# A decoder trunk on one core: the second mixer's background steps of both queues on every second tick

## The chip, the cores and the metric

The kernel runs on one core of one Trainium2 chip. The metric is the device time of one execution in microseconds (us), and lower is better. The time before is the median of three runs.

## The reference, cut to what matters

The reference is one inference step of a two-layer decoder trunk: a Mamba-2 mixer, an MLP with squared ReLU, an HGRN2 mixer, a second MLP. 512 new prompt tokens and 8 sequences of 4 sampled tokens pass through together (544 token columns), width 1024, all in fp32 precision. The change is in the HGRN2 mixer, whose core is this:

```python
proj = u @ w_in                                  # (L, 4 * 1024): q, f, v, g
q = silu(q); k = (1 - lb) * sigmoid(-f)          # 8 heads of 128 x 128
# per token t and head: S_t = diag(f_t) S_{t-1} + k_t v_t^T,  o_t = S_t^T q_t   (in chunks)
o = group_rmsnorm(o) * silu(g)
x = x + o @ w_out
```

The sampled tokens start from a given state for each sequence and return the new one.

## The kernel before

All activations lie transposed: 8 tiles of 128 rows by 544 columns. A weight product is done in three passes (high part by high, high by low, low by high) in fp32r, each in two halves of 272 columns. So one unit of 128 outputs over a depth of 1024 takes 8 x 3 x 2 = 48 matmuls of 272 columns. Weights come by DMA on SyncE's queue into three `raw` buffers; ScalarE (L199) and VectorE (L200) split them into `whi` and `wlo`.

**Foreground and background.** The weight products are the foreground. Whatever else needs TensorE is written as Python generators, and each `yield` in one names how many ticks pass until its next step. `products` calls `tick()` after each 12 matmuls of 272 columns, that is 4 ticks for a unit. A tick takes one off the count of the first generator in each of two queues, and runs a step of it where the count has come to zero or below. `drain(name)` runs what is left of a generator at once, with no foreground between. The first mixer and the first MLP use the same queues before.

**The second mixer** (`hgrn`, L1179). For each of 8 heads `head` makes four units (q, f, v, g). After f it puts `levels(h)` into queue 0. That has eight steps: seven levels with block lengths s = 1, 2, 4, 8, 16, 32, 64 (tile `pa`, matmuls on column strips of 32 or 64 of the array, L1249 and L1268; the first two have an extra pair for the sampled tokens, L1256) and one step `values` (transposes into `pv` and `pvs`). When it ends it puts `states(h)` into queue 1, again eight steps: `pk` (transposes of K), `pS` (chunk states; half a pace until the next step), `pz` (the sampled tokens' old states, column strips of 32, L1362; half a pace until the next), `po` (the outputs, with `pzs`, then squares, mean, Newton steps for the root, scaling), `pn` twice (new states, L1396, added on VectorE in L1399), the store of the new states, and `pt` (transposes of the output, then the gate and the split into the operands `oh`, `ol`). One pace is 1.8 ticks for levels and 1.6 for states.

After the eight heads (128 ticks) comes the output product `pho`: half 0 uses heads 0 to 3 (8 products of 24 matmuls, 16 ticks); then `drain("hs7")` and half 1 with heads 4 to 7 (head 7 is the last operand in each product). Two accumulators (`acc`) take turns in all of these, and four one-bank PSUM tiles (`mx`) serve the background.

A planner turns the program into one order for each engine when the kernel is built: it takes instructions by priority in the order written, except that one whose inputs it does not expect in time is put behind later ones that are ready. `add_to_x` and some others have a higher priority. On the chip each engine then keeps its order.

Of the kernel before, what the change touches and what calls it, by code (L numbers as in the profile page):

```python
# [41 lines left out]


PACE = (1.1, 0.9, 1.4, 0.8)
PACE_LEVELS, PACE_STATES = 1.8, 1.6

U_SSD_IN = 0
U_SSD_OUT = U_SSD_IN + 40
# [53 lines left out]
def trunk(ctx: ExitStack, tc: tile.TileContext, io):  # L102
# [37 lines left out]

    ready = {}
    loaded = {("u", i): t for i, t in enumerate(first)}
    state = {"load": 2, "conv": 0}
    loads = [("u", u) for u in range(U_MLP)]
    jobs = [(("u", u), u) for u in range(U_MLP)]

# [141 lines left out]
    def unit(u):  # L288
        return take(("u", u))
# [3 lines left out]
    queues = [[], []]  # L293

    def tick():
        for q in queues:
            if q:
                q[0][1] -= 1
                while q and q[0][1] <= 0:
                    step(q)  # L300

    def step(q):
        try:
            q[0][1] += next(q[0][0])
        except StopIteration:
            left = q.pop(0)[1]
            if q:
                q[0][1] += left
# [7 lines left out]
    def drain(name):  # L316
        for q in queues:
            while any(e[2] == name for e in q):
                step(q)
# [5 lines left out]
    def products(ps, w, ops, first, last, c0=0, step=P, run=0):  # L325

        n = len(ops)
        order = [(k, j) for k in range(n) for j in range(3)]
        run = run or (4 if "w" in sp else 0)
        if run:  # L330

            order = [(k, j) for k0 in range(0, n, run) for js in ((0, 1), (2,)) for k in range(k0, min(k0 + run, n)) for j in js]
        for i, (k, j) in enumerate(order):
            oh, ol = ops[k]
            a, o = ((w[0], oh), (w[0], ol), (w[1], oh))[j]
            for h in range(2):
                nc.tensor.matmul(  # L337
                    ps[:, h, :HF], block(a, c0 + k * step), o[:, h * HF : (h + 1) * HF],
                    start=(first and i == 0), stop=(last and i == len(order) - 1),
                )  # L340
            if i % 6 == 5:
                tick()

    def acc_tile(name):
        return psb.tile([P, 2, 512], F32, tag="acc", name=name)
# [4 lines left out]
    def v3(t):  # L350
        return t.rearrange("p (a b) -> p a b", a=2)
# [73 lines left out]
    def add_to_x(m, ps, then):  # L425
        with tc.high_priority():
            nc.vector.tensor_tensor(v3(x[m]), ps[:, :, :HF], v3(x[m]), ADD)
        if then is not None:
            then(m)


    def ssd(then):
# [393 lines left out]
        def dt_product():  # L826

            wd = pool.tile([P, KT, NS], F32, tag="E", bufs=2, name="wd")
            nc.vector.tensor_tensor(
                wd, wdt, vec[:, V_NMIX0 : V_NMIX0 + KT].unsqueeze(2).to_broadcast([P, KT, NS]), MUL  # L830
            )
            pd = acc_tile("pd")
            for i in range(2):
                for h in range(2):
                    for c in range(4):
                        k = 4 * i + c
                        nc.tensor.matmul(
                            pd[c * NS : (c + 1) * NS, h, :HF], wd[:, k, :], x[k][:, h * HF : (h + 1) * HF],
                            start=(i == 0), stop=(i == 1), tile_position=(0, c * NS),
                        )  # L840
                tick()
            pdx = pool.tile([P, 640], F32, tag="xs", bufs=5, name="pdx")
            nc.vector.tensor_tensor(v3(pdx[:, :T]), pd[:, :, :HF], v3(rb), MUL)
            nc.gpsimd.tensor_copy(
                pdx[:, T:640].rearrange("p (a b) -> p a b", b=NS), pdx[:, NP_:T].unsqueeze(1).to_broadcast([P, 3, NS])
            )
            return pdx
# [122 lines left out]
    def mlp(name, plan, v0, then, last=False):  # L970
# [105 lines left out]
        def seventh(name_, u):  # L1076
# [11 lines left out]
            for k in range(4):  # L1088
                oh, ol = ops_[name_, k]
                for j, (w, o) in enumerate(((hi, oh), (hi, ol), (lo, oh))):  # L1090
                    nc.tensor.matmul(  # L1091
                        ps, block(w, k * P), o, start=(name_ in ("p1", "p2", "q7") and k == 0 and j == 0),
                        stop=(k == 3 and j == 2), skip_group_check=name_ in ("n6", "n5", "p3", "q4"),
                    )
            tick()
            release(1)
            keep = {"p1": "s1", "n6": "sv", "n5": "sw"}.get(name_)
# [81 lines left out]
    def hgrn(then):  # L1179
# [263 lines left out]

        sc = slice(NP_, T)
        u = U_HGRN_IN
        ops = [[pool.tile([P, T], F32R, tag=f"o{c}{h}", bufs=1, name=f"o{c}{h}") for c in "hl"] for h in range(8)]
        for h in range(8):
            head(u, h)
            u += 4
        for half in range(2):  # L1450
            if half:
                drain("hs7")
            for mp in range(4):
                w = unit(u)
                u += 1
                for i in range(2):
                    ps = acc_tile(f"pho{half}_{mp}_{i}")
                    products(ps, w, ops[4 * half : 4 * half + 4], True, True, i * P, 2 * P)
                    add_to_x(2 * mp + i, ps, then if half == 1 else None)
        es.close()  # L1460

    CH = (0, 91, HF - 91)
# [47 lines left out]
    ssd(pre_norm(V_NMLP0))  # L1510
    mlp("m0", plans[0], V_NMLP0, pre_norm(V_NMIX1))
    hgrn(pre_norm(V_NMLP1))
    mlp("m1", plans[1], V_NMLP1, last_norm, True)

# [111 lines left out]
def _build(arrays):  # L1626
    import concourse.bacc as bacc

    nc = bacc.Bacc("TRN2", target_bir_lowering=False, num_devices=1)
    io = {n: nc.dram_tensor(f"in_{n}", v.shape, mybir.dt.from_np(v.dtype), kind="ExternalInput").ap() for n, v in arrays.items()}  # L1630
    for n, s in _OUT.items():
        io[n] = nc.dram_tensor(f"out_{n}", s, F32, kind="ExternalOutput").ap()
    with tile.TileContext(nc) as tc:
        trunk(tc, io)
    return nc
# [22 lines left out]
```

## Time and profile before

| | |
|---|---|
| median of 3 runs | 1518.04 us (1516.65 to 1519.53) |
| the profiled execution's own time | 1517.97 us |
| its span | 1516.2 us |
| busy share of the span | PE 99%, PEld 95%, DVE 83%, ACT 58%, POOL 12% |
| granted TensorE clock, mean | 0.994 of 2.4 GHz |
| the second mixer (first product to last) | 816.05 to 1147.80 us |

PE is TensorE's matmul side and PEld its weight loads, DVE is VectorE, ACT ScalarE, POOL GpSimd, SP SyncE. L337 is a line of the kernel. Matmuls are pipelined and their records overlap, so the time that TensorE spends on something is read from the distances between starts. In the rows `ps<-uh,whi x2` is one pair of foreground matmuls; pairs that follow each other start 0.25 us apart.

### The profile page before, as it was taken

The page shows a single profiled execution, that of the slowest core. Times are in us where ns is not written, and L with a number is a line of the kernel's source. Part 1 is how long each engine was busy: PE and PEld are TensorE (multiplying, and loading weights), DVE is VectorE, ACT ScalarE, POOL GpSimd, SP SyncE. Part 2 cuts the span into 40 slices and gives each one's busy share as a digit, 9 for nine tenths or more (in the row PEclk, how much of TensorE's full clock was granted, in tenths as well). Part 3 has the DMA queues.
Part 4 walks back from the last instruction along what each step waited for, and adds up shares of the span by engine and source line. Part 5 has one row for each costly group of instructions (what it writes and reads, how often), then busy time and mean ns, then how long its engine had stood idle before and what let it go on. Part 6 is the DMA issues. An engine that isn't in the chain of part 4 may idle for free. (4 is left out here: it accounts for less than half of the span.)

```text
span 1516.2 us, 33224 instructions
## 1 busy us (share of the span) xinstructions
PE 1495.4 (99%) x13144; PEld 1440.3 (95%) x13144; DVE 1261.5 (83%) x2532; ACT 882.3 (58%) x1740; POOL 188.0 (12%) x273
## 2 busy tenths in 40 slices
PE   9999999999999999999999999999999999999997
PEld 7998989898999999999999999999999999999996
DVE  7879798978777989888898788888877989888895
ACT  5685766757346658575676333333336758576673
POOL 3211011110012111111110000000002111111101
PEclk9999999999999999999999999999999999999998
DMA  6366557574466667564754232233228666575741
GB/s 199 106 192 169 148 140 203 130 223 115 114 178 135 141 161 183 145 183 131 191 131 130 74 99 87 87 98 105 86 86 202 133 168 180 140 181 140 184 123 66
DMA packets 105789, 215.46 MB, mean 142 GB/s; under 512 B 16481, under 2 KB 36865, under 8 KB 105633
## 3 DMA queue, kind: packets, MB, share of 16 engines
q1 hardware_dynamic: 81328, 170.24, 34.7%
q0 software_dynamic: 23040, 41.95, 17.3%
q8 instruction: 103, 1.69, 0.5%
q10 hardware_dynamic: 1264, 1.14, 0.2%
q14 instruction: 54, 0.43, 0.1%
HBM read 196.12 MB, written 17.18 MB: 141 GB/s over the span
## 5 line engine op out<-in xcount | busy, mean ns | idle before, releaser
L199 ACT CAST whi<-raw 128x512 fp32r<-128x512 f32 x194 | 119.4, 617 | 212.0 <-PE ps L337 154.6
L200 DVE TENSOR_TENSOR wlo<-raw,whi 128x512 fp32r<-128x512 f32 x194 | 133.8, 691 | 30.8 <-ACT whi L199 28.0
L188 POOL DMA_DIRECT2D v<-in_W x94 | 83.0, 1038 | 463.6 <-DVE fl_p L200 134.0
L337 PE MATMUL ps<-uh_s,whi 128*128 128x272 f32 x576 | 124.3, 297 | 2.5 <-DVE BC L518 2.4
L337 PE MATMUL ps<-ul_s,whi 128*128 128x272 f32 x576 | 120.2, 290 | 0.0
L337 PE MATMUL ps<-uh,whi 128*128 128x272 f32 x512 | 112.6, 300 | 0.0
L337 PE MATMUL ps<-ul,whi 128*128 128x272 f32 x512 | 106.5, 289 | 0.0
L337 PE MATMUL ps<-uh,wlo 128*128 128x272 f32 x512 | 106.3, 289 | 0.0
L337 PEld LDWEIGHTS ps<-uh_s,whi 128*128 128x128 f32 x576 | 90.5, 189 | 8.5 <-issue 6.9
L337 PEld LDWEIGHTS ps<-ul_s,whi 128*128 128x128 f32 x576 | 90.9, 189 | 0.2
L200 DVE TENSOR_TENSOR fl_p<-raw,fh_p 128x512 fp32r<-128x512 f32 x94 | 64.1, 689 | 28.9 <-ACT fh_p L199 25.3
L337 PE MATMUL ps<-uh_s,wlo 128*128 128x272 f32 x576 | 86.4, 290 | 0.0
L337 PEld LDWEIGHTS ps<-uh,whi 128*128 128x128 f32 x512 | 80.8, 189 | 3.7 <-issue 1.4
L337 PEld LDWEIGHTS ps<-ul,whi 128*128 128x128 f32 x512 | 80.4, 189 | 0.0
L337 PEld LDWEIGHTS ps<-uh,wlo 128*128 128x128 f32 x512 | 80.0, 188 | 0.0
L199 ACT CAST fh_p<-raw 128x512 fp32r<-128x512 f32 x94 | 57.6, 620 | 37.9 <-PE pp L1091 19.9
L337 PEld LDWEIGHTS ps<-uh_s,wlo 128*128 128x128 f32 x576 | 78.1, 190 | 1.1 <-issue 0.8
L223 ACT CAST whi<-raw 128x512 fp32r<-128x512 f32 x66 | 40.6, 618 | 49.4 <-PE ps L337 19.6
L511 DVE SCALAR_TENSOR_TENSOR cacc<-pre,vh,cacc 128x568 f32<-128x568 f32 x72 | 57.8, 803 | 7.6 <-ACT cacc L509 7.1
L337 PE MATMUL po<-yh,whi 128*128 128x272 f32 x256 | 55.5, 297 | 1.2 <-ACT yh L199 1.2
L1091 PE MATMUL pp<-m_tl,fh_n 128*128 128x272 f32 x192 | 55.3, 288 | 0.0
L1091 PE MATMUL pc_q<-m_th,fh_q 128*128 128x272 f32 x192 | 55.3, 288 | 0.0
(480 smaller groups left out, 5156.0 us busy)
## 6 DMA issues: line engine op xcount, KB each, us to landing
raw<-in_W SPq DMA_DIRECT2D x175, 512.0 KB, 4.0
v<-in_W SPq DMA_DIRECT2D x94, 256.0 KB, 4.1
v<-in_W POOLq DMA_DIRECT2D x94, 256.0 KB, 5.6
wlo<-in_W POOLq DMA_DIRECT2D x66, 256.0 KB, 6.2
a<-in_W SPq DMA_DIRECT2D x47, 256.0 KB, 4.3
w<-cum_d SPq DMA_DIRECT2D x16, 512.0 KB, 6.9
st<-in_ssm_in SPq DMA_DIRECT2D x16, 512.0 KB, 4.6
out_ssm_s<-st SPq DMA_DIRECT2D x16, 512.0 KB, 6.6
```

Source lines behind the costliest of these rows:

```text
L188: nc.gpsimd.dma_start(raw[:, c : c + 512], io["W"][u + 1][:, :512], accum_op=ADD)
L199: nc.scalar.copy(hi, raw)
L200: (eng or nc.vector).tensor_tensor(lo, raw, hi.bitcast(F32), SUB)
L223: nc.scalar.copy(hi[a], c)
L337: nc.tensor.matmul(ps[:, h, :HF], block(a, c0 + k * step), o[:, h * HF : (h + 1) * HF], start=(first and i == 0), stop=(last and i == len( ...
L511: nc.vector.scalar_tensor_tensor(acc, pre[:, i : i + 568], vh[:, wc + 24 * i : wc + 24 * i + 1], acc, MUL, ADD)
L1091: nc.tensor.matmul(ps, block(w, k * P), o, start=(name_ in ("p1", "p2", "q7") and k == 0 and j == 0), stop=(k == 3 and j == 2), skip_group ...
```

## The change

The two paces become 2 ticks. `state` gets a count of ticks, and a beat: `tick()` still counts down each queue at every tick, but runs steps only when the count of ticks, which goes on from the kernel's start, is a multiple of the beat. The beat is 1 outside, and 2 from the first head to the end of the output product. `drain` is as before.

```diff
-PACE_LEVELS, PACE_STATES = 1.8, 1.6
+PACE_LEVELS, PACE_STATES = 2, 2
...
-    state = {"load": 2, "conv": 0}
+    state = {"load": 2, "conv": 0, "ticks": 0, "beat": 1}
...
     def tick():
+
+        state["ticks"] += 1
         for q in queues:
             if q:
                 q[0][1] -= 1
-                while q and q[0][1] <= 0:
+                while q and q[0][1] <= 0 and state["ticks"] % state["beat"] == 0:
                     step(q)
...
         u = U_HGRN_IN
+        state["beat"] = 2
...
                     add_to_x(2 * mp + i, ps, then if half == 1 else None)
+        state["beat"] = 1
         es.close()
```

## Rows read from the trace of the kernel before

**Rows 1.** Who TensorE waited for in the whole execution (us in total, times, longest).

```profile
PE po L337 <- ACT yh L199: 1.2, 2, 0.6
PE po L337 <- DVE yl L200: 0.6, 1, 0.6
PE pp L1091 <- ACT sw L1101: 0.3, 1, 0.3
```

**Rows 2.** Busy time of each engine in the second mixer; the last three numbers are granted clock, DMA share and GB/s.

```profile
816.05:1147.80 331.75, 331.66 (x3925) 311.55 (x3924) 268.93 (x734) 120.85 (x249) 9.19 (x23) 1.00 0.30 96
```

**Rows 3.** The chain of work around head 1's first level: start, us, what.

```profile
859.79 3.71 PE ps L337 x28
863.51 0.58 PE pa L1249 x32
```

**Rows 4.** TensorE in order of time around one level step (s = 16) that stands alone: start, us, line, tile.

```profile
882.88 0.41 PE L337 MATMUL ps<-uh,wlo 128*128 128x272 f32 x2
883.22 0.46 PE L1249 MATMUL pa<-q,K 128*32 128x32 f32 x32
883.61 0.52 PE L337 MATMUL ps<-uh,whi 128*128 128x272 f32 x2
883.96 0.41 PE L337 MATMUL ps<-ul,whi 128*128 128x272 f32 x2
```

**Rows 5.** The same around the first level (s = 1) of head 0, which stands alone: last pair ahead, first matmuls, second pair behind.

```profile
834.81 0.41 PE L337 MATMUL ps<-uh,wlo 128*128 128x272 f32 x2
835.16 0.65 PE L1249 MATMUL pa<-q,K 128*32 128x64 f32 x32
...
836.19 0.41 PE L337 MATMUL ps<-ul,whi 128*128 128x272 f32 x2
```

**Rows 6.** The same around `pz` of head 0, which stands alone.

```profile
868.39 0.41 PE L337 MATMUL ps<-uh,wlo 128*128 128x272 f32 x2
868.73 0.65 PE L1362 MATMUL pz<-hst,qm 128*32 128x128 f32 x16
...
869.39 0.50 PE L337 MATMUL ps<-uh,whi 128*128 128x272 f32 x2
869.73 0.41 PE L337 MATMUL ps<-ul,whi 128*128 128x272 f32 x2
```

**Rows 7.** The same around a first level and a `pz` that stand together.

```profile
900.55 0.41 PE L337 MATMUL ps<-uh,wlo 128*128 128x272 f32 x2
...
901.47 0.60 PE L1362 MATMUL pz<-hst,qm 128*32 128x128 f32 x13
...
902.42 0.41 PE L337 MATMUL ps<-ul,whi 128*128 128x272 f32 x2
```

**Rows 8.** The last pair ahead and the second pair behind, first of a level (s = 4) with `po` right behind it, then of a `po` that stands alone.

```profile
870.73 0.41 PE L337 MATMUL ps<-uh,wlo 128*128 128x272 f32 x2
...
874.24 0.41 PE L337 MATMUL ps<-ul,whi 128*128 128x272 f32 x2
...
903.43 0.41 PE L337 MATMUL ps<-uh,wlo 128*128 128x272 f32 x2
...
906.36 0.42 PE L337 MATMUL ps<-ul,whi 128*128 128x272 f32 x2
```

**Rows 9.** The start of the mixer, TensorE and VectorE: the norm's second step, the first evacuation that needs it, and the first pair of the third unit.

```profile
826.42 1.20 PE L382 MATMUL hn_pr<-ident,nwr 128*128 128x128 f32 x10
...
828.21 0.72 DVE L1228 TENSOR_TENSOR qz<-ps,hn_rb 128x544 f32<-128x544 f32 x1 [0.46 <-ACT hn_rb L385]
...
830.54 0.42 PE L337 MATMUL ps<-uh,whi 128*128 128x272 f32 x2
```

**Rows 10.** The last head's output around the border of the two halves: TensorE, then VectorE, then ScalarE, each in order of time.

```profile
1115.44 0.52 PE L337 MATMUL pho<-oh,whi 128*128 128x272 f32 x2
...
1117.06 0.39 PE L1396 MATMUL pn<-vm,kq 128*128 128x512 f32 x1
1117.29 0.41 PE L337 MATMUL pho<-oh,whi 128*128 128x272 f32 x2
...
1122.04 0.60 PE L1406 MATMUL pt<-ident,o 128*128 128x128 f32 x4
...
1122.74 0.52 PE L337 MATMUL pho<-oh,whi 128*128 128x272 f32 x2
...
1115.91 0.82 DVE L1386 TENSOR_REDUCE oms<-o 128x5 f32<-128x640 f32 x1 [1.26 <-ACT o L1384]
...
1120.23 0.69 DVE L1389 TENSOR_TENSOR o<-po,nwr 128x512 f32<-128x512 f32 x1
...
1121.51 0.33 DVE L1392 TENSOR_SCALAR o<-pzs,nwr 32x128 f32<-32x128 f32 x1
...
1124.04 0.73 DVE L1410 SCALAR_TENSOR_TENSOR g<-pt,vec,g 128x512 f32<-128x512 f32 x1
...
1124.96 0.65 ACT L199 CAST oh<-g 128x544 fp32r<-128x544 f32 x1 [2.36 <-DVE g L1411]
```

**Rows 11.** SyncE's queue at the same place: the last store of new states and the next weight load.

```profile
1124.13 1.42 SPq L1401 DMA_DIRECT2D out_hgrn_s<-hst  x1
1131.11 0.33 SPq L178 DMA_DIRECT2D raw<-in_W  x1
```

**Rows 12.** Busy time of each engine and the granted clock around the end of the first mixer (columns as in rows 2).

```profile
435.00:445.00 10.00, 8.69 (x48) 7.82 (x49) 5.94 (x10) 4.39 (x7) 4.22 (x5) 0.83 0.91 243
```

## The prediction

> **What bounds the kernel.** I read the page first, then who TensorE waited for, then the stage that the change touches, and there TensorE in order of time. No line in the list of TensorE's waits belongs to the second mixer; some of the list that lie nearest before it are in [rows 1]. In the mixer TensorE is busy for 331.66 of 331.75 us at a clock of 1.00, VectorE for 268.93 and ScalarE for 120.85 [rows 2]. So the mixer's time is the sum of what stands in TensorE's order. Of that the foreground is 40 units of 48 matmuls (8 heads of 4, and the output product as 8) = 1920 matmuls, or 960 pairs of 0.25 us: 240 us. The other 90 us or so are background steps. The change deletes no instruction. It can move the time in three ways only: what TensorE loses where it changes between foreground and background, a new wait of TensorE, or a weight that comes late.
>
> The planner already keeps TensorE from waiting: head 1's first level is due 12 matmuls after the level before it, and stands behind 28 [rows 3], since its inputs are not there sooner.
>
> **Which steps meet, before and after.** This is counted from the code. Before the mixer 449 ticks have passed: 217 in the first mixer (two units of 4; one in the product for dt; 36 units of 4; 32 output products of 2) and 232 in the MLP (8 up and 8 down units of 4, and 24 pairs with 7 products of one each). 449 is odd, so the beat falls on the mixer's odd ticks. Before the change, two heads take 32 ticks and interrupt the foreground 23 times, because paces of 1.8 and 1.6 drift against each other: `pk`, `pS`, `po` or `pn` meet a level at times, and `pz` stands alone in one head and with the first level in the next. After it each head is the same, eight visits in 16 ticks: (s1, pk), (s2, pS), (s4, pz, po), (s8, pn), (values, pn), (s16, store), (s32, pt), (s64). `pz` and `po` fall together because half a pace is now one tick, and steps run at every second. So 16 visits for two heads instead of 23.
>
> **What a visit costs.** From the last pair ahead to the second pair behind, less two pairs (0.50):
> - A level alone: 883.96 - 882.88 - 0.50 = 0.58, of which 0.09 is ahead of its first matmul (883.22 - 882.88 - 0.25) and 0.10 behind the first pair after it [rows 4].
> - A level with `po` behind it: 874.24 - 870.73 - 0.50 = 3.01; `po` alone 906.36 - 903.43 - 0.50 = 2.43 [rows 8]. 0.58 + 2.43 = 3.01: meeting saves nothing. The change from column strips to the whole array is paid at `po` instead of at the foreground.
> - First level alone 0.88 [rows 5], `pz` alone 0.84 [rows 6], the two together 902.42 - 900.55 - 0.50 = 1.37 [rows 7]: meeting saves 0.35. Both work on column strips.
> - Behind `pz` the foreground's first pair takes 869.73 - 869.39 - 0.25 = 0.09 too long [rows 6]. With `po` behind it that is saved.
>
> The Trainium skill (TensorEngine Tiling, Key Properties) states that a change of tiling mode drains TensorE, while another tile of the same mode does not. The rows agree: 0.09 and 0.10 around a level, nothing saved with an untiled neighbour, something with a tiled one. By that rule alone the gain would be one pair of changes in every second head, 0.19 x 3.5 = 0.7 us.
>
> **Gain.** After the change `pz` meets s4 in every head, before it met a level in every second. The meeting saves between 0.19 (0.09 + 0.10) and 0.35, and the border to `po` another 0.09: 0.28 to 0.44 per head, against 0.35 / 2 = 0.17 before. Over 7 heads that is (0.11 to 0.27) x 7 = 0.8 to 1.9 us. I take **-1.3 us**. The other meetings count as nothing, by rows 8.
>
> **The start.** The norm's second step `hn_pr` was due at tick 6 and is now run at tick 7, 12 matmuls or 1.5 us later. The third unit needs the first unit's accumulator, which `qz` frees. It ended at 828.21 + 0.72 = 828.93 and the third unit began at 830.54 [rows 9]. 1.5 us later it ends at 830.43: the slack falls from 1.6 us to 0.1. I take **+0.1**, from 0 to 0.7 (one ScalarE cast of 0.65, as in rows 10, ahead of the copies).
>
> **The border of the halves.** Here is the cost. Head 7's states start at tick 139 instead of 136, and go at 2 ticks a step. Before, `po` ran at tick 140, both `pn` in ticks 141 and 143, and only the store and `pt` were left for `drain`. Now `pz` and `po` run at tick 143, one tick ahead of the border, and `drain` has `pn`, `pn`, the store and `pt` with no foreground between them. The operand of head 7 was ready at 1124.96 + 0.65 = 1125.61, which is 10.2 us after the foreground came back behind `po` at 1115.44 [rows 10]. In this stretch VectorE also did its other work. Without it the chain is: 0.47 until the reduction, 0.85 for it, 2.4 for the scalar and 11 Newton steps, 1.0 for the two scalings, 0.9 for the transposes, 0.9 for the gate, 0.9 for the cast, about 7.4 us (estimated from the same stretch). What TensorE can do meanwhile: 12 foreground matmuls (1.5), two `pn` (1117.29 - 1117.06 = 0.23 each), the first 18 matmuls of both open accumulators, which need heads 4 to 6 only (36 x 0.125 = 4.5), and `pt` (0.8): 7.3 us. So TensorE waits between 0.1 (bare chain) and 2.9 us (VectorE as loaded as before). VectorE is 81% busy in the mixer [rows 2] and the eight adds of `pn` fall into the same stretch, but their order is the planner's. I take **+1.5**. Late next is the split of x behind the first products of half 1, which has its own accumulators' time as cover.
>
> **What else moves.** On SyncE's queue the store of new states and the state loads move by a few ticks, with weight loads behind them. The last store waits for the last `pn` add; the next weight load came 5.6 us after that store was through (1124.13 + 1.42 to 1131.11) [rows 11], so a store 2 to 3 us later is covered. Without cover it would cost its delay once. GpSimd is busy for 9.19 us of 331.75 [rows 2] and its copies keep their distance to their readers. Four `mx` tiles are enough for (s4, pz, po with pzs); where one is not free, the planner puts foreground there, as in rows 3. `po` behind `pz` needs ScalarE's copy for `pzs` only, 1.6 us later. Each of these: 0.
>
> **Sum.** -1.3 + 0.1 + 1.5 = +0.3 us. The profiled execution's 1517.97 becomes 1518.3; its median is 1518.04, which makes 1518.3 as well.
>
> **Rivals.**
> - *Slower: the border is not covered.* If the planner leaves `pn`, `pn`, `pt` in the order written, TensorE waits for the scaled output: 1121.84 - 1115.44 = 6.4 us after `po`, less 1.5 and 0.5, is 4.4, and behind it only one accumulator's 2.3 us covers a chain of some 3. That is about 4.5 to 5 us. Such a pause can also cost clock: around 435 to 445 us, where TensorE waited 1.2 + 0.6 us [rows 1], the granted clock was 0.83 in the mean [rows 12], which is part of it at the lower level of 1.2 GHz, and 10 x 0.17 = 1.7 us of work lost. The Trainium skill (TensorE: Matmul & The Clock Gate, HAM oscillation) names this as the mechanism: idle gaps bring the gate back to half rate; rows 12 agree. -1.3 + 4.8 + 1.7 = +5.2: 1523 us. It decides from a wait of 4.4 us. Against it: in rows 3 the planner did fill.
> - *Faster: each visit saved is worth a whole pair of changes.* 7 visits fewer for two heads, 24.5 in all, at 0.19 is 4.7 us: 1513.4 us. Against it speak rows 8. Half of it would do to be faster, with the border covered.
> - *It does nothing that can be seen*: both terms under 0.5 us, 1517.5 to 1518.5. That lies within the forecast.
>
> **Numbers.** Forecast (small gain, small wait) 0.75; the slower rival 0.15; the faster one 0.10. The bound of what can be told is 0.2%, 3.0 us. Slower by more needs a wait above 4.3 us, or one of 2.6 with lost clock; faster by more needs three times my gain and no wait. So faster 0.09, same 0.75, slower 0.16. Range: from 1518.04 - 1.9 less 1.0 for the runs' own scatter (1516.65 to 1519.53), 1515.2, to 1518.04 - 0.8 + 0.7 + 2.9 + 1.0 = 1521.8; I stop at 1522.2, which takes in the start of the slower rival.
>
> **What would show it.** In the changed profile: 8 visits in each head; (s4, pz, po) at 3.4 to 3.6 us where the three alone make 0.58 + 0.84 + 2.43 = 3.85; a first pause of TensorE between 828 and 832 of at most 0.7; a pause of 0 to 3 us at the border behind a run of first products of both accumulators; the mixer's stretch at 332 us. The prediction is wrong if TensorE waits inside the heads (for `zi` or a PSUM tile), if the clock falls at the border, or if other stages change by more than 1 us.

## The result: slower by 0.3%, and the profile after

The changed kernel takes 1522.55 us (median of 7 runs, 1521.54 to 1526.24) against 1518.04 us before (the median of seven runs too, and the same as of the three ahead of the prediction). The ratio is 1.0032, with a 95% interval of 1.0022 to 1.0042. That lies just above the range (1522.2), between the forecast and the slower rival, "the border is not covered" (1523): the rival's lost clock came, its long wait did not. The profiled execution took 1522.55 us with a span of 1520.8 us and a mean granted clock of 0.993.

Line numbers of the changed kernel are two higher than before: the products are L339, the levels L1251, `pz` L1364, `po` L1377 and L1379, the adds of `pn` L1401, the scaling L1391, `pt` L1408, the gate L1412.

Where TensorE waited in the whole execution: of the lines that name steps of the second mixer there were none before [rows 1], and now there are three (engine, line, who was waited for: us in total, times, longest).

```profile
PE pho L339 <- ACT oh L199: 1.5, 1, 1.5
PE pt L1408 <- DVE o L1391: 1.3, 1, 1.3
PE pn L1398 <- ACT vt L1315: 0.4, 1, 0.4
```

The first two stand at the border of the halves. This is TensorE there in order of time, after the change (start, us, line, tile; in brackets how long it was idle before, and for whom):

```profile
1118.51 0.65 PE L1364 MATMUL pz<-hst,qm 128*32 128x128 f32 x16
...
1121.24 0.40 PE L1382 MATMUL pzs<-vs,sats 32*32 32x128 f32 x2
1121.58 0.73 PE L1398 MATMUL pn<-vm,kq 128*128 128x512 f32 x2
1122.14 0.41 PE L339 MATMUL pho<-oh,whi 128*128 128x272 f32 x2
...
1126.41 0.41 PE L339 MATMUL pho<-oh,wlo 128*128 128x272 f32 x2
1128.15 0.63 PE L1408 MATMUL pt<-ident,o 128*128 128x128 f32 x4 [1.33 <-DVE o L1391]
1128.71 0.24 PE L1409 MATMUL pts<-ident,o 32*128 32x32 f32 x1
1130.46 1.27 PE L339 MATMUL pho<-oh,whi 128*128 128x272 f32 x4 [1.51 <-ACT oh L199]
1131.53 0.66 PE L339 MATMUL pho<-ol,whi 128*128 128x272 f32 x2
```

Three things are to be seen. Both `pn` follow `pzs` at once: no foreground stands between `po` and the drain. The 36 first products of both open accumulators (18 pairs, the first at 1122.14, the last at 1126.41) do fill a part, as the prediction had it. Then TensorE waits for the scaled output and for the operand `oh`, and behind the second wait a pair takes 0.45 us and more (1131.53 to 1131.98, where the next one starts) instead of 0.25. The windows show why (busy time of PE, PEld, DVE, ACT, POOL; then clock, DMA share, GB/s):

```profile
1118.00:1130.00 12.00, 9.62 (x83) 8.20 (x81) 8.45 (x30) 2.78 (x7) 0.00 (x0) 1.00 0.26 92
1130.00:1134.00 4.00, 3.54 (x15) 3.31 (x16) 1.87 (x3) 1.22 (x3) 0.00 (x0) 0.57 0.00 0
1134.00:1152.50 18.50, 18.50 (x150) 18.50 (x149) 15.21 (x24) 11.90 (x21) 0.00 (x0) 1.00 0.39 125
```

For 4 us after the waits the clock granted was 0.57 in the mean, most of it at the lower level of 1.2 GHz: 4 x 0.43 = 1.7 us of work lost. Before, the whole mixer had 1.00 [rows 2]. So the border costs 1.33 + 1.51 + 1.7 = 4.5 us.

From the first product to the start of the last `pho` matmul the mixer takes 334.02 us, before 330.74: +3.28. (The end at 1147.80 in the table of before lies behind that, in the first products of the next stage.) The stretch can be cut in two where the heads end and the border begins, at the last pair ahead of head 7's `pS`: up to there both kernels have run the same background steps. These are the first product and that pair, first before, with what follows the pair, then after:

```profile
816.08 0.41 PE L337 MATMUL ps<-uh,whi 128*128 128x272 f32 x2
...
1108.13 0.42 PE L337 MATMUL pho<-oh,wlo 128*128 128x272 f32 x2
1108.38 1.05 PE L1352 MATMUL pS<-vt,kt 128*128 128x128 f32 x8
1109.19 0.50 PE L337 MATMUL pho<-oh,whi 128*128 128x272 f32 x2
1109.53 0.41 PE L337 MATMUL pho<-ol,whi 128*128 128x272 f32 x2
```
```profile
817.58 0.41 PE L339 MATMUL ps<-uh,whi 128*128 128x272 f32 x2
...
1114.27 0.41 PE L339 MATMUL pho<-oh,wlo 128*128 128x272 f32 x2
```

After the change 24 more pairs of foreground, 6.0 us, stand ahead of it, since `pS` comes four ticks later. So the heads have changed by (1114.27 - 817.58) - 6.0 - (1108.13 - 816.08) = -1.36 us, which is what the visits saved, and the rest, with the border in it, by 3.28 + 1.36 = +4.64, near the 4.5 above.

The other 1.3 us of the difference between the two profiled executions (4.58 in all) stand elsewhere. In the first mixer a step that began at 160.42 us before begins at 161.88, although TensorE's order up to there is the same in both. The windows there, before and then after (columns as above):

```profile
145.00:170.00 25.00, 21.58 (x163) 20.92 (x164) 18.10 (x40) 9.65 (x18) 2.01 (x4) 0.93 0.79 243
```
```profile
145.00:170.00 25.00, 21.57 (x151) 20.92 (x151) 16.69 (x38) 8.55 (x16) 2.01 (x4) 0.86 0.79 243
```

TensorE is busy for the same time and gets less done in it, by a clock of 0.86 against 0.93: 25 x 0.07 = 1.75 us. In eight other kernels, none of which changes that part, the same step began between 159.85 and 164.51 us. Up to that step the order of all 1180 of TensorE's matmuls is the same in the ten traces. That is scatter between executions and no effect of the change. How much of the loss in the other runs stands outside the mixer, no run shows. So kernels are compared below by the ratio of their times and by the stretch of the second mixer alone.

### The profile page after: what moved, and what is told of

Read it like the earlier page. It is cut to its first block, busy times and chain, and to the rows that moved or that the text cites. A ratio compares the mean times of both kernels' runs of the same rounds, so it can differ in the third digit from the quotient of the medians.

```text
span 1520.8 us, 33217 instructions
## 1 busy us (share of the span) xinstructions
PE 1496.7 (98%) x13144; PEld 1441.0 (95%) x13144; DVE 1267.8 (83%) x2532; ACT 883.0 (58%) x1740; POOL 191.0 (13%) x273
## 5 line engine op out<-in xcount | busy, mean ns | idle before, releaser
L339 PE MATMUL ps<-uh_s,whi 128*128 128x272 f32 x576 | 124.6, 298 | 2.5 <-DVE BC L520 2.4
L339 PE MATMUL ps<-ul_s,whi 128*128 128x272 f32 x576 | 120.7, 291 | 0.0
L339 PE MATMUL ps<-uh,whi 128*128 128x272 f32 x512 | 110.7, 297 | 0.0
L339 PE MATMUL ps<-ul,whi 128*128 128x272 f32 x512 | 106.0, 288 | 0.0
L339 PE MATMUL ps<-uh,wlo 128*128 128x272 f32 x512 | 105.8, 288 | 0.0
L339 PEld LDWEIGHTS ps<-uh_s,whi 128*128 128x128 f32 x576 | 90.7, 190 | 8.5 <-issue 6.9
L339 PEld LDWEIGHTS ps<-ul_s,whi 128*128 128x128 f32 x576 | 91.3, 190 | 0.3
L339 PE MATMUL ps<-uh_s,wlo 128*128 128x272 f32 x576 | 87.3, 292 | 0.0
L339 PEld LDWEIGHTS ps<-uh,whi 128*128 128x128 f32 x512 | 80.3, 188 | 3.0 <-issue 1.2
L339 PEld LDWEIGHTS ps<-ul,whi 128*128 128x128 f32 x512 | 80.2, 188 | 0.0
L339 PEld LDWEIGHTS ps<-uh,wlo 128*128 128x128 f32 x512 | 80.1, 188 | 0.0
L339 PEld LDWEIGHTS ps<-uh_s,wlo 128*128 128x128 f32 x576 | 79.0, 192 | 1.1 <-issue 0.8
L339 PE MATMUL po<-yh,whi 128*128 128x272 f32 x256 | 55.4, 297 | 1.2 <-ACT yh L199 1.2
```

Of the source, the lines that this page charges most:

```text
L339: nc.tensor.matmul(ps[:, h, :HF], block(a, c0 + k * step), o[:, h * HF : (h + 1) * HF], start=(first and i == 0), stop=(last and i == len( ...
```

## The experiments

Four kernels ran together on one chip, four others together on another, each with runs of the kernel before beside them (medians there 1518.18 and 1517.90 us). The mixer's stretch is from each profiled execution, as the difference to 330.74 us. "Heads" is the part of it up to the last pair ahead of head 7's `pS`, reckoned as above, and "rest" what remains. "Waits" are TensorE's at the border as the profile lists them, "lost clock" the stretch at a lower clock behind them times what was missing of 1.00.

| | median us | ratio (95%) | mixer | heads | rest | waits | lost clock |
|---|---|---|---|---|---|---|---|
| the change | 1522.55 | 1.0032 (1.0022 to 1.0042) | +3.28 | -1.36 | +4.64 | 1.3 + 1.5 | 1.7 |
| e1_beat_only | 1518.01 | 0.9998 (0.9989 to 1.0007) | -0.71 | -0.92 | +0.21 | none | none |
| e2_border_only | 1523.69 | 1.0032 (1.0020 to 1.0043) | +5.20 | +0.03 | +5.17 | 1.3 + 1.5 + 0.2 | 1.7 |
| e3_odd | 1521.96 | 1.0021 (1.0013 to 1.0030) | +1.81 | -0.69 | +2.50 | 1.2 + 0.3 + 0.2 | none |
| e4_fill | 1521.67 | 1.0021 (1.0012 to 1.0030) | +1.99 | -1.36 | +3.35 | 0.3 | none |
| e5_quick_end | 1516.55 | 0.9989 (0.9980 to 0.9997) | -1.51 | -1.71 | +0.20 | none | none |
| e6_pace_only | 1523.10 | 1.0034 (1.0021 to 1.0047) | +4.47 | +0.89 | +3.58 | 1.2 + 0.3 | 1.7 |
| e7_out_first | 1518.49 | 1.0004 (0.9996 to 1.0013) | +0.41 | -1.37 | +1.78 | 0.3 + 0.3 + 0.2 | none |
| e8_border_24 | 1521.17 | 1.0022 (1.0013 to 1.0030) | +2.58 | +0.02 | +2.56 | 1.3 + 0.3 | none |

Two cautions. Mixer, waits and clock come from one execution of each kernel, and that of e3 is the slowest of its 11 runs, that of e8 the fastest; whether the clock falls in the others is not seen. And a wait is listed from the end of the record before it (0.41 us for a pair whose successor could start after 0.25), so it can cost 0.16 us more than listed.

The theory (T in the expectations): the visits save a little, and the late steps of the last head at the border cost more. The rivals: the beat itself costs something, inside the heads; or the time is lost to the place of the border steps by parity alone.

**The beat without the new paces.** On the changed kernel:

```diff
-PACE_LEVELS, PACE_STATES = 2, 2
+PACE_LEVELS, PACE_STATES = 1.8, 1.6
```

> The beat of the change with the old paces (1.8 and 1.6). Steps still meet on every second tick, but head 7 goes as fast as before: its po runs at tick 140 and only one pn and pt are left for the drain. Theory T (all of the loss is the border of the two halves, the meetings themselves gain about 1.1 us as measured between the start and the border): no wait of TensorE at the border, about 1516.5 us, 1.5 below the kernel before. Rival V (steps that meet cost time, by PSUM tiles or longer chains): 1518.5 to 1520 us, and TensorE waits inside the heads.

The mixer becomes 0.71 us shorter and TensorE has no wait at the border. The whole time is that of before and not the 1516.5 us that was expected: 0.7 us is less than the runs can tell. The beat as such costs nothing that they show, and in the heads it saves 0.92 us.

**The border alone.** On the kernel before, with no beat (the new pace stands in every `yield` of `states`):

```diff
 def states(h, d):
+    pace = 4 if h == 7 else PACE_STATES
...
-    yield PACE_STATES
+    yield pace
```

> The kernel before, with one thing changed: the pace of head 7's states alone is 4 ticks instead of 1.6, so that its po falls on the border and both pn, the store and pt are left for the drain. No beat, no other pace. Theory T: the border costs 4.6 us as in the changed kernel (two waits of about 2.8 us together and a fall of the clock), 1522.6 us. Rival V: the border is only part, 1519 to 1520.5 us.

Only the last head's states are late, and the whole loss is there: nothing in the heads, and the same two waits with a lower clock behind them. The waits:

```profile
PE pho L337 <- ACT oh L199: 1.5, 1, 1.5
PE pt L1407 <- DVE o L1390: 1.3, 1, 1.3
```

The window behind them (columns as above):

```profile
1130.00:1136.00 6.00, 5.44 (x28) 4.91 (x29) 4.65 (x7) 3.33 (x6) 0.00 (x0) 0.72 0.10 35
```

This settles the place. Waits of 3.0 and 6 x 0.28 = 1.7 us of clock make 4.7 of its +5.20.

**One tick earlier.** The changed kernel with its count of ticks begun at 1, so that the beat falls on the mixer's odd ticks, where the prediction had put it:

```diff
-    state = {"load": 2, "conv": 0, "ticks": 0, "beat": 1}
+    state = {"load": 2, "conv": 0, "ticks": 1, "beat": 1}
```

> The changed kernel with its count of ticks started at one, so that the beat falls on the mixer's odd ticks, as the prediction had it: pz and po of head 7 run one tick (12 matmuls, 1.5 us) ahead of the border. Theory T: the two waits shrink from 2.8 to about 1.3 us. If the clock then stays up, 1522.55 - 1.5 - 1.6 = 1519.4 us; if it still falls, 1521.0. Rival V: 1522.5 as the changed kernel.

12 foreground matmuls now stand between `po` and the first `pn`, as the prediction had it. Of the waits 1.7 us are left, near the +1.5 that it took, and in this execution the clock held. The waits:

```profile
PE pho L339 <- ACT oh L199: 1.2, 1, 1.2
PE pho L339 <- DVE x L429: 0.3, 1, 0.3
PE pts L1409 <- DVE o L1394: 0.2, 1, 0.2
```

The window behind them:

```profile
1130.00:1135.00 5.00, 3.22 (x20) 2.38 (x20) 3.42 (x7) 1.32 (x3) 0.00 (x0) 1.00 0.27 111
```

The mixer is 1.5 us shorter than with the change as made. That is not the cover alone: the listed waits fall by 1.1 us, the clock that held is worth 1.7, and the heads gain 0.7 us less. The rest, +2.50, is more than the 1.7 listed, since read between starts the three waits cost 2.1 us, and 0.26 us more goes to a pair behind the operand that waits for its low part `ol`. The median is only 0.6 us below that of the change, with runs from 1518.82 to 1524.42; it is above both values expected of the theory and nearest to the rival's. So parity is a part of the loss, and not all of it.

**Work in place of the wait.** The changed kernel with 22 matmuls, whose result is overwritten, ahead of the last head's second `pn`; they are work beyond the reference's:

```diff
 pn = mx(f"pn{h}_{i}")
+for _ in range(22 if h == 7 and i == 1 else 0):
+    nc.tensor.matmul(pn[:, :HF], ops[4][0][:, :P], ops[4][0][:, :HF], start=True, stop=True)
```

> The changed kernel with 22 extra matmuls of 272 columns (2.8 us, their result is overwritten) ahead of head 7's second pn, so that TensorE works where it waited. The output is unchanged. Theory T with the lost clock as part of it: the waits are filled and cost nothing more, the clock stays at 1.00, 1522.55 - 1.6 = 1520.9 us. If the lower clock has another cause than the waits: 1522.5. If the waits were not what limits: 1525.3, the 2.8 us on top.

22 matmuls are 2.75 us of TensorE, as much as the two waits. With them in that place the waits are gone but for 0.3, and the clock behind is whole (the window there):

```profile
1130.00:1135.00 5.00, 4.68 (x38) 4.46 (x37) 4.42 (x8) 3.01 (x5) 0.00 (x0) 1.00 0.18 40
```

The mixer is 1.3 us shorter than with the change, though TensorE does 2.75 us more work. What came back is as much as the clock. The separation isn't perfect: the planner also put `pt` behind 20 instead of 36 foreground matmuls.

**No late border.** The changed kernel, with the last head's levels and the last two heads' states at a pace of 1.4 and the beat back at 1 from there:

```diff
 def levels(h, QQ, K, f, d):
+    pace = 1.4 if h == 7 else PACE_LEVELS
+    if h == 7:
+        state["beat"] = 1
...
 def states(h, d):
+    pace = 1.4 if h > 5 else PACE_STATES
```

> The changed kernel with its border undone: heads 0 to 5 as changed, but from head 7's levels on the beat is 1 again, head 7's levels have a pace of 1.4 and the states of heads 6 and 7 one of 1.4, so that head 7's pt runs ahead of the drain. Theory T (the border is all of the loss): no wait of TensorE there, the mixer takes about as long as in e1, 0.5 to 1.2 us less than before; 1517.5 us, which is the same as the kernel before. Rival V (the meetings in the heads cost time): 1519.5 us or more.

No wait at the border, the mixer 1.51 us shorter, and the median 1516.55 us: 0.9989 of before (0.9980 to 0.9997), so slightly faster than the kernel before, whose median beside it is 1517.90, and 1 us below what was expected. TensorE is not idle in the stretch of the border (the window there):

```profile
1115.00:1125.00 10.00, 10.00 (x80) 9.79 (x80) 7.42 (x17) 1.79 (x3) 0.00 (x0) 1.00 0.37 130
```

**The paces without the beat.** The changed kernel without one line:

```diff
-        state["beat"] = 2
```

> The changed paces of 2 and 2 without the beat: steps run at every tick as they come due, so pz and po stay apart and po of head 7 runs one tick (12 matmuls) ahead of the border, with both pn, the store and pt for the drain. Theory T: waits at the border of about 1.4 us as in e3, the mixer 1.5 to 2 us longer than before, with the clock falling in some executions; 1520 us. Were it the beat that costs: 1518.

This was missed. The waits are 1.5 us as with the odd beat, but the clock fell here (the window behind them):

```profile
1130.00:1135.00 5.00, 5.00 (x28) 4.77 (x28) 4.09 (x6) 3.00 (x5) 0.00 (x0) 0.66 0.18 46
```

That is 1.7 us. `pz` and `po` are a tick apart again, and the heads lose 0.89 us: `pz` now stands alone in every head, at 871.93 - 870.60 - 0.50 = 0.83 us in the first, where before it met the first level in every second head. 1.5 + 1.7 + 0.9 = 4.1 of +4.47. So waits of 1.2 + 0.3 us stood once with a lower clock behind them and once (e3, with 0.2 more) without.

**The output ahead of the new states.** In the changed kernel the last head's `pt`, with gate and split, is put ahead of its two `pn`, their adds and the store (these are in `news`):

```diff
+def news():
+...
+if h < 7:
+    yield from news()
 pt = mx(f"pt{h}")
...
+if h == 7:
+    yield from news()
```

> The changed kernel, with head 7's pt step put ahead of its two pn steps, so that the eight adds of pn on VectorE no longer stand between the Newton steps of the output's chain. Theory T with VectorE's queue as what makes the chain long: the adds took about 0.13 us each from the chain, 1 us in all; the waits fall from 2.8 to 1.8 us, and the clock may stay up: 1520 to 1521.5 us. If the chain's own latency is all: 1522.5.

It was better than expected: the time of before, 1518.49 us, and 2.9 us less in the mixer than with the change, though `pz` and `po` run at the same late tick. Of the 2.9 us 1.7 are the clock, which did not fall in this execution; the other 1.2 are what is left for shorter waits (0.8 listed instead of 2.8; the short ones cost more than they are listed with). VectorE's order ahead of the scaling is what differs. VectorE with the change (as above, some rows), where `oms` is the mean of the squares, `nwr` the root and `o<-po,nwr` the scaling:

```profile
1122.11 0.35 DVE L1401 SCALAR_TENSOR_TENSOR hst<-hst,T,pn 128x128 f32<-128x128 f32 x1 [1.84 <-PE pn L1398]
1122.38 0.81 DVE L1388 TENSOR_REDUCE oms<-o 128x5 f32<-128x640 f32 x1
1123.11 0.34 DVE L1401 SCALAR_TENSOR_TENSOR hst<-hst,T,pn 128x128 f32<-128x128 f32 x1
...
1126.51 0.69 DVE L200 TENSOR_TENSOR wlo<-raw,whi 128x512 fp32r<-128x512 f32 x1 [0.33 <-ACT whi L199]
1127.12 0.16 DVE L367 SCALAR_TENSOR_TENSOR nwr<-nwt,nwr 128x5 f32<-128x5 f32 x1
1127.31 0.69 DVE L1391 TENSOR_TENSOR o<-po,nwr 128x512 f32<-128x512 f32 x1
1127.92 0.33 DVE L1394 TENSOR_SCALAR o<-pzs,nwr 32x128 f32<-32x128 f32 x1
```

And with the output first:

```profile
1120.15 0.82 DVE L1388 TENSOR_REDUCE oms<-o 128x5 f32<-128x640 f32 x1 [1.77 <-ACT o L1386]
...
1123.29 0.69 DVE L1391 TENSOR_TENSOR o<-po,nwr 128x512 f32<-128x512 f32 x1
1123.90 0.33 DVE L1394 TENSOR_SCALAR o<-pzs,nwr 32x128 f32<-32x128 f32 x1
...
1125.62 0.85 DVE L1402 SCALAR_TENSOR_TENSOR hst<-hst,T,pn 128x128 f32<-128x128 f32 x3
```

From the start of the reduction to the end of the scaling it is 1127.92 + 0.33 - 1122.38 = 5.9 us with the change, and 1123.90 + 0.33 - 1120.15 = 4.1 us with the adds behind. With the change the adds, and a weight split that waits for ScalarE, stand between the small steps of the root; with the output first neither does. The edit moves both `pn`, their adds and the store together, and with them the split, so what the adds alone are worth is not shown.

**More distance, the same order.** As e2_border_only, with 3 in place of 4, so that 24 foreground matmuls, 3 us, stand between `po` and the drain:

```diff
-    pace = 4 if h == 7 else PACE_STATES
+    pace = 3 if h == 7 else PACE_STATES
```

> As e2 (the kernel before, only head 7's states slowed), but with a pace of 3 instead of 4: po runs 24 matmuls (3 us) ahead of the border instead of on it, and the same steps (two pn, the store, pt) are left to the drain. Theory T by the measured chain: 3 us more cover than e2, whose waits were 2.8 us: no wait at the border, 1518 to 1518.5 us. If the drain itself costs (both pn at once, order of the steps) and not the distance: 1520 us or more.

Missed as well: a wait of 1.3 us for `oh` stays, and the time is 1521.17 us. The mixer is 2.6 us shorter than in e2, of which 1.7 are the clock. VectorE's order took up much of the distance:

```profile
1123.61 0.68 DVE L1390 TENSOR_TENSOR o<-po,nwr 128x512 f32<-128x512 f32 x1
1124.21 0.33 DVE L1393 TENSOR_SCALAR o<-pzs,nwr 32x128 f32<-32x128 f32 x1
1124.47 1.62 DVE L1400 SCALAR_TENSOR_TENSOR hst<-hst,T,pn 128x128 f32<-128x128 f32 x6
1126.02 0.73 DVE L1411 SCALAR_TENSOR_TENSOR g<-pt,vec,g 128x512 f32<-128x512 f32 x1
1127.13 0.69 DVE L200 TENSOR_TENSOR wlo<-raw,whi 128x512 fp32r<-128x512 f32 x1 [0.38 <-ACT whi L199]
1127.74 0.24 DVE L1412 SCALAR_TENSOR_TENSOR g<-pts,vec,g 128x32 f32<-128x32 f32 x1
```

And ScalarE's cast of the operand behind it:

```profile
1128.02 0.64 ACT L199 CAST oh<-g 128x544 fp32r<-128x544 f32 x1 [0.92 <-DVE g L1412]
```

Six adds stand ahead of the gate (1124.47 to 1126.02), and a weight split with its wait ahead of the gate's last part (1127.13). Between the small steps of the root stand two more weight splits and an add to x (1120.43, 1121.71, 1122.35), so that from the reduction (1118.65) to the end of the scaling it is again 5.9 us. From the foreground's return behind `po` (1118.19) to the operand (1128.66) it is 10.5 us, as before the change (10.2). So distance alone didn't decide here. What counted is what VectorE had been given between the output's steps, against the foreground that was left.

## Why the prediction was wrong, and where it was right

Two steps of the prediction failed: the cover that it counted at the border wasn't there, and lost clock stood in its sum at nothing.

**The parity was miscounted.** The tick of the first mixer's product for dt stands inside a loop of two, so it ticks twice: 450 ticks precede the mixer, not 449. The beat falls on even ticks, and `pz` and `po` of the last head run at tick 144, which is the border itself. The 12 matmuls, 1.5 us, that the prediction counted as cover between `po` and the drain aren't there. e3_odd gives them back, and the listed waits fall from 2.8 to 1.7 us. But with 1.0021 of before it is not at the forecast of +0.3 us either, so the miscount alone doesn't account for the miss.

**The chain was as long as taken; the cover was short.** From the end of `pzs` (1121.58, where `pn` starts) to the operand (1129.76 + 0.64) it took 8.8 us. The prediction had 7.4 to 10.2, and its +1.5 is 8.8 less its cover of 7.3. With 1.5 us less cover the wait becomes 3.0, and 1.33 + 1.51 = 2.8 us were listed. So the wait was mis-sized by the cover and not by VectorE. That VectorE's order makes the chain longer than need be is so as well: with the output first it takes 6.7 us (1119.68 to 1125.73 + 0.65).

**The clock was left out of the sum.** The prediction names three ways in which the change can move the time, and the clock is none of them. It stood in the slower rival and among the signs of being wrong, as 1.7 us, read from a place with waits of 1.2 + 0.6 us [rows 1, 12]. It came, with 1.7 us. The condition under "Numbers", "one of 2.6 with lost clock", was met with 2.8. The slower rival itself was met by half: the planner did not leave the steps in the order written, 36 products stand ahead of `pt`, and the wait was 2.8 us instead of 4.5 to 5.

With these two terms the sum is -1.4 + 2.8 + 1.7 = +3.1 us, and the mixer's stretch shows +3.28. That would have made about 1521.2 us, inside the range. The other 1.3 us of the two profiled executions stand outside the mixer, as said; whether the medians differ by so much more through scatter alone stays open.

**The gain was right.** Predicted -1.3 us (0.8 to 1.9); the heads show -1.36, with a wait of 0.4 us of `pn` for a transpose's copy, which was not foreseen, already paid in it. The visit of the third level, `pz` and `po` was to take 3.4 to 3.6 us, with 3.85 for the three apart [rows 4, 6, 8]. It is there, TensorE after the change:

```profile
875.74 0.41 PE L339 MATMUL ps<-uh,wlo 128*128 128x272 f32 x2
876.08 0.46 PE L1251 MATMUL pa<-q,K 128*32 128x32 f32 x32
876.36 0.67 PE L1364 MATMUL pz<-hst,qm 128*32 128x128 f32 x16
...
879.11 0.40 PE L1382 MATMUL pzs<-vs,sats 32*32 32x128 f32 x2
879.44 0.52 PE L339 MATMUL ps<-uh,whi 128*128 128x272 f32 x2
879.79 0.41 PE L339 MATMUL ps<-ul,whi 128*128 128x272 f32 x2
```

879.79 - 875.74 - 0.50 = 3.55 us, 0.30 less than apart; over 7 heads and against the 0.17 of before that is 0.9 of the -1.36. e6_pace_only, where `pz` meets nothing, loses 0.89 in the heads. So the faster rival, which priced every visit saved at 0.19 us, falls: no kernel saves more than 1.7 us in the heads. One reading behind the price was off. The 0.10 us behind a level was put down to the column strips; behind `pS`, which uses the whole array, the first pair is as late (1109.53 - 1109.19 - 0.25 = 0.09, shown above), and it is not behind `pn` (1117.29 to 1117.54, 0.25). `pS` is an fp32 product and `pn` an fp32r one like the foreground. The 0.09 ahead of a level is not there ahead of `pS` (1108.13 to 1108.38).

**The start cost nothing.** With an even beat the norm's second step runs at tick 6, as before, and TensorE has no wait there. With the odd beat (e3_odd) it runs at tick 7, and no wait is listed there either. **SyncE's queue, GpSimd and the PSUM tiles** were costed at nothing, and no wait of TensorE points to them. Behind the first products of half 1 the prediction saw cover enough; TensorE waits 0.2 to 0.3 us there for an add to x in five of the experiments, and not with the change.

## What to carry to other kernels

Where background work is drained at a border, follow the last item's chain in the order that each engine was given, and count what other queued work (adds, weight splits) stands between its steps; putting the result that is waited for ahead of work that nobody waits for took the ratio from 1.0032 to 1.0004 here, 3 us more distance from 1.0032 to 1.0022. Count the ticks of a parity in the loops themselves, or cost both parities. A change that saves 1.4 us by merging steps over a whole stage can lose 4.6 at the one place where the foreground ends: keep the last steps of the stage early, as e5_quick_end does, and price the clock behind a pause together with the pause.

## What the runs showed of the hardware

Two waits of 1.3 and 1.5 us were followed by 4 us at a granted clock of 0.57, 1.7 us of work on top of 2.8 us of waiting. With 2.75 us of useless matmuls in that place the clock stayed at 1.00 in the execution traced, and the mixer was 1.3 us shorter. In e2_border_only the first pairs behind the pause still stood 0.25 us apart (1131.50 to 1131.75) and later ones 0.45 (1133.35 to 1133.80): the clock fell behind the pause and not with it. The Trainium skill (TensorE: Matmul & The Clock Gate, HAM oscillation) says that idle gaps bring the gate back to half rate; its example has longer gaps than these, and the rows agree in the change, e2_border_only and e6_pace_only. Waits of about 1.5 us stood with a clock of 0.66 in one kernel and of 1.00 in two others (e6_pace_only; e3_odd and e8_border_24), so the size of a pause alone didn't tell here whether the clock falls. And the same instructions in the same order took up to 4.7 us more or less by 160 us into the execution (159.85 to 164.51); in the two compared above the granted clock differs there, 0.93 and 0.86.
